# A deeper ring for expert rows: nine places, eight fetches asked ahead, and the dot written over its own rows

## The chip, the cores and the metric

The kernel runs on one core of a Trainium2 chip. Its five engines are told by the names of the profile: PE (TensorE), DVE (VectorE), ACT (ScalarE), POOL (GpSimd) and SP (SyncE); each works through its own list of instructions in order. The metric is the device time of one execution in microseconds (us), lower is better. The kernel before takes 1699.54 us (median of three runs, 1698.48 to 1712.32).

## The reference

Two layers work on 256 tokens of width 1024. Each layer has a mixer (gated linear attention beside spatial gating, one input projection, one output projection), a residual norm, an expert retrieval and another residual norm:

```python
h = _layer_norm(x, ln_in_g, ln_in_b)
for l in range(DEPTH):                                  # 2
    h = _layer_norm(ALPHA * h + _mixer(h, ...), ln1_g[l], ln1_b[l])
    h = _layer_norm(ALPHA * h + _peer(h, ...), ln2_g[l], ln2_b[l])

def _peer(x, ...):       # per token: 8 heads x top 16 = 128 experts of 16384
    ...                  # q = x @ wq, product keys, two rounds of top_k
    ub = jnp.take(u_tab, ib, axis=0)
    act = jax.nn.gelu(jnp.einsum('td,tkd->tk', xb, ub), approximate=False)
    vb = jnp.take(v_tab, ib, axis=0)
    return jnp.einsum('tk,tkd->td', gb * act, vb)
```

For each token and each of its 128 experts, a row u of 1024 numbers is fetched and multiplied with the token (a dot), the result goes through GELU and a gate, and a row v of 1024 numbers, times that weight, is added up.

## The kernel before

**The expert stream.** The 256 tokens are two blocks (b = 0, 1) of 128, one token to a partition. With two layers that makes four stretches of 128 expert steps, K = 128 and N = 512 steps in all, in the order (layer 0, b 0), (layer 0, b 1), (layer 1, b 0), (layer 1, b 1). Step k of a stretch handles the k-th expert of all 128 tokens:
- `gather` (line 726): one indirect DMA, issued by POOL, fetches for each token a row of 2048 floats (u beside v, 8 KB a partition, 1 MB in all) into a `uv` tile. The tiles are a ring of UVBUFS = 7 places.
- `dot` (line 733): one DVE instruction multiplies the u half with the token's row of `h` and sums it into `dots`; the products themselves go to a tile `junk` that nothing reads.
- `weigh` (lines 739 to 742): three ACT instructions make GELU, the gate, and `dg`, a diagonal matrix of the weights.
- the product (line 791): TensorE multiplies `dg` with the v half, two halves of 512 columns (x2 in the lists of the order, x4 in the profile), adding up in two `bank_acc` banks over the 128 steps.

A place of the ring is free for a new gather when its product is done.

**The side work.** Beside the steps of one stretch the kernel computes what the next stretch needs, a Python generator `side(n)`: the residual norm of the stretch that has just ended, the whole mixer of the next layer for that block (weights `raw` come over SP's DMA queue, ACT and DVE split each into two parts, `whi` on line 142 and `wlo` on line 147), then `ask`: the retrieval's queries, keys and rounds of top 16, nearly all of it small DVE instructions (lines 603 to 678). Each `yield` of a generator names a cost; the loop takes pieces until the cost passes PACE, then goes on to the next step. The last stretch has only a norm beside it.

**What sets the order.** DVE, ACT and PE run in the order in which the loop writes their instructions. In step i the loop writes: the gather of expert i + AHEAD - 1 (AHEAD = 5, so i + 4), the product of expert i - 2, the dot of expert i, the weighing of expert i - 1, then the pieces of side work. POOL's list holds the gathers and a few small powers for the norms (lines 161 and 215, `rs` and `rrs`), in the order of the program too.

Of the kernel before, what the change touches and what calls it, by code (L numbers as in the profile page):

```python
# [8 lines left out]
F32 = mybir.dt.float32  # L9
# [5 lines left out]
OP = mybir.AluOpType  # L15
# [6 lines left out]
D = 1024  # L22
# [11 lines left out]
NCAND = sum(na * nb for _, na, nb in RECTS)  # L34
NEG = -3.0e38
RAW, HI, LO = 4, 3, 2
UVBUFS, AHEAD = 7, 5
PACE = (1.65, 1.36, 1.36, 1.5)
OUTS = (4, 5, 6, 7, 0, 1, 2, 3)
HH = 2  # L40
# [59 lines left out]
class Trunk:  # L100
# [470 lines left out]
    def run(self):  # L571
        nc, a, sm = self.nc, self.a, self.sm
        with self.tc.tile_pool(name="peer", bufs=1) as pp:
# [108 lines left out]
            def ask(l, b, feed):  # L682

                S = pp.tile([128, PH, 2, NK], F32, name="S", tag="S")
                banks = [None]

                def query(i):
                    if i % 2 == 0:
                        banks[0] = self.bank("a")
                    p = self.wide(b, *feed.get(), banks[0][:, i % 2 * 256:(i % 2 + 1) * 256])  # L690
                    feed.split()
                    yield
                    s = pp.tile([128, 128], F32, name="f_half", tag="f_half", bufs=2)
                    nc.scalar.copy(s, p[1])  # L694
                    yield
                    q = pp.tile([128, 128], F32, name="qp", tag="qp", bufs=2)
                    nc.vector.tensor_tensor(q, p[0], s, op=OP.add)  # L697
                    yield
                    p2 = self.bank("b")[:, :128]
                    nc.tensor.matmul(p2, lhsT=q, rhs=kt[:, l, i % 2], start=True, stop=True)  # L700
                    yield
                    nc.scalar.copy(S[:, i // 2, i % 2], p2)
                    yield
                    h, half = divmod(i, 2)
                    top16((S[:, h, half], v16[:, h, half], i16[:, h, half]))
                    if i % (2 * HH) == 2 * HH - 1:
                        yield
                        yield from retrieve(l, h // HH)
                live = []
                todo = [query(i) for i in range(16)]  # L710
                while todo or live:
                    for w in list(live):
                        try:
                            next(w)
                        except StopIteration:
                            live.remove(w)
                    if todo:
                        w = todo.pop(0)
                        next(w)
                        live.append(w)  # L720
                    yield 2.9


            def gather(eid, k):
                uv = pp.tile([128, 2 * D], F32, name="uv", tag="uv", bufs=UVBUFS)
                nc.gpsimd.indirect_dma_start(out=uv, out_offset=None, in_=a["uv"],  # L726
                                             in_offset=bass.IndirectOffsetOnAxis(ap=eid[:, k:k + 1], axis=0),
                                             bounds_check=L * NK * NK - 1, oob_is_err=False)
                return uv

            def dot(b, k, uv, dots):
                junk = pp.tile([128, D], F32, name="junk", tag="junk")
                nc.vector.scalar_tensor_tensor(junk, uv[:, :D], 1.0, self.h[:, b], op0=OP.mult, op1=OP.mult,  # L733
                                               accum_out=dots[:, k:k + 1])

            def weigh(k, ex, dots):

                c = dots[:, k:k + 1]
                nc.scalar.activation(c, c, AF.Gelu)  # L739
                nc.scalar.mul(c, c, ex[:, k:k + 1])  # L740
                dg = pp.tile([128, 128], F32, name="dg", tag="dg", bufs=3)
                nc.scalar.mul(dg, self.ident, c)  # L742
                return dg

            chosen, ready = [], set()
            def side(n, done):

                if n == 0:
                    yield from asked
                    nc.sync.dma_start(self.h[:, 1], a["x"][128:256, :])  # L750
                    feed = self.feed_of(0)
                    yield 0.1
                    yield from self.input_block(1)
                    yield from self.front(pp, 0, 1, feed)
                    yield from ask(0, 1, feed)
                elif n < 3:
                    b = n - 1
                    feed = self.feed_of(1)
                    yield from self.residual_block(done, b, V_LN2)
                    if b == 0:  # L760
                        self.layer_constants(pp, 1)
                    yield from self.front(pp, 1, b, feed)
                    yield from ask(1, b, feed)
                else:
                    yield from self.output_block(done, 0, V_LN2 + V_LAYER)

            with self.tc.manual_schedule(engines=ORDERED):
                for _ in self.input_block(0):
                    pass
                for _ in self.front(pp, 0, 0, feed):  # L770
                    pass
                asked = ask(0, 0, feed)
                while (0, 0) not in ready:
                    next(asked)


                K = PH * TK
                N = NB * L * K
                uvs, dgs = {}, {}
                work, debt, acc = None, 0.0, None  # L780
                for i in range(N + 2):
                    for j in range(0 if i == 0 else i + AHEAD - 1, min(i + AHEAD, N)):
                        while (j // K, j % K // KH) not in ready:
                            next(work)
                        uvs[j] = gather(chosen[j // K][0], j % K)
                    if i > 1:
                        m = i - 2
                        if m % K == 0:
                            acc = [self.bank("acc") for _ in range(2)]
                        for hf in range(2):  # L790
                            nc.tensor.matmul(acc[hf], lhsT=dgs[m], rhs=uvs[m][:, D + hf * 512:D + (hf + 1) * 512],  # L791
                                             start=m % K == 0, stop=m % K == K - 1)
                        del dgs[m], uvs[m]
                    if i < N:
                        dot(i // K % NB, i % K, uvs[i], chosen[i // K][2])
                    if 0 < i <= N:
                        dgs[i - 1] = weigh((i - 1) % K, *chosen[(i - 1) // K][1:])
                    if i == 0 or (i > 2 and i % K == 1 and i < N):
                        for _ in work or []:
                            pass  # L800
                        work, debt = side(i // K, acc), 0.0
                    if work:
                        debt += PACE[min(i // K, 3)]
                        while debt > 0:
                            c = next(work, work)
                            if c is work:
                                break
                            debt -= c or 1.5
                for _ in self.output_block(acc, 1, V_LN2 + V_LAYER):
                    pass  # L810

# [86 lines left out]
```

## Time and profile before

| what | value |
|---|---|
| median of three runs | 1699.54 us |
| the profiled execution's own time | 1692.46 us |
| its span in the profile | 1690.7 us |
| PE, DVE, ACT, POOL busy | 85%, 71%, 47%, 36% of the span |
| moved by DMA | 636.60 MB, 377 GB/s in the mean |
| share of the 16 DMA engines: gathers, weights | 78.3%, 15.3% |
| gathers, dots, products | 512 each |

The busy shares are means over stages with different limits. A row of the windows view tells what an engine did in one stretch of time; a row of the waits view tells who kept an engine idle. Times in them count from the start of the span.

### The profile page before, as it was taken

Reading aid. Unit: us, or ns where it says so; the run is one execution under the profiler, and the core shown is the slowest. Engines: PE = TensorE matmul, PEld = TensorE weight load, DVE = VectorE, ACT = ScalarE, POOL = GpSimd, SP = SyncE. Lnnn points to the kernel's source line nnn. Section 1 sums busy time; section 2 is a strip of 40 time slices with the busy share of each in tenths; the row PEclk is TensorE's granted clock in tenths of the full one; section 3 lists DMA queues with packets and bytes.
Section 4 is the critical chain, followed back from the end, with each engine's and each line's share of the span. In section 5 each row is a group of like instructions: output and inputs, shape, how many; then the busy total and the mean of one; then the engine's idle time right before and its main releaser. Section 6 shows DMA issues by size and latency. Waiting matters only on the chain.

```text
span 1690.7 us, 17829 instructions
## 1 busy us (share of the span) xinstructions
PE 1430.4 (85%) x4544; PEld 749.1 (44%) x4544; DVE 1204.0 (71%) x2898; ACT 794.7 (47%) x2106; POOL 614.1 (36%) x542
## 2 busy tenths in 40 slices
PE   7887699989878889989887798989977887777776
PEld 5675255646533455445543354545543332222222
DVE  6778977767998667666898566766899654444444
ACT  5643465654544565544444374544444433333332
POOL 0002343444324343444334343444324433333331
PEclk9976999999899999999999898999989989999999
DMA  7647999999989999999989999999989999999996
GB/s 234 224 143 300 347 390 396 416 417 419 404 330 364 392 418 391 419 419 419 396 353 386 402 399 363 418 419 419 419 320 361 409 372 421 422 421 422 421 421 255
DMA packets 102409, 636.60 MB, mean 377 GB/s; under 512 B 11634, under 2 KB 12436, under 8 KB 36772
## 3 DMA queue, kind: packets, MB, share of 16 engines
q0 software_dynamic: 73872, 537.49, 78.3%
q1 hardware_dynamic: 28436, 97.98, 15.3%
q8 instruction: 37, 0.61, 0.1%
q14 instruction: 64, 0.52, 0.1%
HBM read 634.38 MB, written 1.05 MB: 376 GB/s over the span
## 4 chain that ended last, share of the span: by engine, by line
DVE 28%; DMA 24%; issue 19%; PE 14%; POOL 12%; ACT 2%; POOLq 1%; DVEq 0%; SPq 0%; ACTq 0%
DMA uv<-uv,eid 23%; POOL uv L726 11%; DVE junk L733 10%; PE bank_acc L791 7%; PE bank_a L153 5%; DVE wlo L147 3%; DVE i L605 2%; DVE v L603 2%; PE bank_b L179 1%; DVE S L608 1%; DVE sums L650 1%; POOLq L726 1%; DVE pos L605 1%; DVE sums L651 1%; ACT whi L142 1%
## 5 line engine op out<-in xcount | busy, mean ns | idle before, releaser
L791 PE MATMUL bank_acc<-uv,dg 128*128 128x512 f32 x2048 | 1012.3, 629 | 199.0 <-ACT dg L742 187.7
L726 POOL DMA_INDIRECT uv<-uv,eid x512 | 595.8, 1164 | 917.8 <-PE bank_acc L791 599.1
L733 DVE SCALAR_TENSOR_TENSOR junk<-uv,h 128x1024 f32<-128x1024 f32 x512 | 626.8, 1224 | 369.6 <-DMA uv<-uv,eid 364.6
L791 PEld LDWEIGHTS bank_acc<-uv,dg 128*128 128x128 f32 x2048 | 375.6, 196 | 723.4 <-ACT dg L742 383.9
L739 ACT ACTIVATE dots<-dots 128x1 f32<-128x1 f32 x512 | 103.3, 202 | 561.1 <-DVE junk L733 556.6
L147 DVE TENSOR_TENSOR wlo<-raw,whi 128x1024 fp32r<-128x1024 f32 x180 | 218.9, 1219 | 35.0 <-issue 16.9
L742 ACT ACTIVATE dg<-ident,dots 128x128 f32<-128x128 f32 x512 | 205.6, 402 | 38.5 <-PE bank_acc L791 21.9
L142 ACT CAST whi<-raw 128x1024 fp32r<-128x1024 f32 x180 | 187.4, 1044 | 42.9 <-DMA raw<-wmix 23.6
L740 ACT ACTIVATE dots<-dots,ex 128x1 f32<-128x1 f32 x512 | 150.8, 295 | 16.6
L153 PE MATMUL bank_a<-whi,x 128*128 128x512 f32 x384 | 137.2, 465 | 6.4 <-ACT f_sr L520 4.8
L153 PE MATMUL bank_a<-x,whi 128*128 128x256 f32 x672 | 118.9, 325 | 9.3 <-ACT f_half L694 6.1
L153 PEld LDWEIGHTS bank_a<-x,whi 128*128 128x128 f32 x672 | 98.2, 213 | 24.6 <-issue 9.8
L153 PEld LDWEIGHTS bank_a<-whi,x 128*128 128x128 f32 x384 | 72.7, 192 | 48.0 <-issue 27.4
L153 PE MATMUL bank_a<-x,wlo 128*128 128x128 f32 x672 | 91.1, 282 | 0.0
L153 PEld LDWEIGHTS bank_a<-x,wlo 128*128 128x128 f32 x672 | 89.5, 206 | 0.0
L179 PE MATMUL bank_b<-vecs,ident 16*128 16x512 f32 x96 | 58.9, 752 | 23.8 <-DVE f_at L408 11.9
L694 ACT COPY f_half<-bank_a 128x128 f32<-128x128 f32 x64 | 17.0, 265 | 113.6 <-DVE qp L697 109.1
L153 PE MATMUL bank_a<-wlo,x 128*128 128x512 f32 x192 | 66.6, 401 | 2.0 <-DVE wlo L147 1.9
L700 PEld LDWEIGHTS bank_b<-kt,qp 128*128 128x128 f32 x128 | 26.0, 214 | 40.6 <-issue 17.1
L179 PEld LDWEIGHTS bank_b<-vecs,ident 16*128 16x128 f32 x96 | 19.5, 219 | 55.2 <-issue 30.2
L153 PEld LDWEIGHTS bank_a<-wlo,x 128*128 128x128 f32 x192 | 36.3, 191 | 13.3 <-DVE wlo L147 5.2
L733 DVE DVE_READ_ACCUMULATOR junk<-uv,h 128x1 f32 x512 | 42.1, 82 | 0.0
(137 smaller groups left out, 761.6 us busy)
## 6 DMA issues: line engine op xcount, KB each, us to landing
raw<-wmix SPq DMA_DIRECT2D x180, 512.0 KB
uv<-uv,eid POOLq DMA_INDIRECT x512
h<-x SPq DMA_DIRECT2D x2, 512.0 KB
out<-h SPq DMA_DIRECT2D x4, 256.0 KB
f_cM<-gm POOLq DMA_DIRECT2D x1, 576.0 KB
f_sw<-sgwT SPq DMA_DIRECT2D x2, 256.0 KB
f_msk<-gmask SPq DMA_DIRECT2D x1, 320.0 KB
kt<-kT SPq DMA_DIRECT2D x2, 128.0 KB
```

The source lines that it names most:

```text
L142: self.nc.scalar.copy(hi, raw)
L147: self.nc.vector.tensor_tensor(lo, raw, hi.bitcast(F32), op=OP.subtract)
L153: self.nc.tensor.matmul(out, lhsT=l, rhs=r, start=start and i == 0, stop=stop and i == n - 1)
L179: self.nc.tensor.matmul(p, lhsT=self.ident[0:16, row:row + 1].to_broadcast([16, 128]), rhs=self.vecs[:, hf * 512:(hf + 1) * 512], start=Tr ...
L603: nc.vector.max(v[:, r], vals)
L605: nc.vector.max_index(i[:, r], v[:, r], vals)
L726: nc.gpsimd.indirect_dma_start(out=uv, out_offset=None, in_=a["uv"], in_offset=bass.IndirectOffsetOnAxis(ap=eid[:, k:k + 1], axis=0), boun ...
L733: nc.vector.scalar_tensor_tensor(junk, uv[:, :D], 1.0, self.h[:, b], op0=OP.mult, op1=OP.mult, accum_out=dots[:, k:k + 1])
L739: nc.scalar.activation(c, c, AF.Gelu)
L740: nc.scalar.mul(c, c, ex[:, k:k + 1])
L742: nc.scalar.mul(dg, self.ident, c)
L791: nc.tensor.matmul(acc[hf], lhsT=dgs[m], rhs=uvs[m][:, D + hf * 512:D + (hf + 1) * 512], start=m % K == 0, stop=m % K == K - 1)
```

## The change

The ring gets nine places, and in step i the loop writes the gather of expert i + 7, where it was i + 4. The dot writes its products over the u half that it has just read, and the tile `junk` is gone. The product of expert i - 1 is now written at the end of step i, behind the side work, where the product of i - 2 was written at the start of step i before. The side work of a stretch starts one step after the stretch's first dot; before, that held for all but the first stretch, whose side work started with its first dot.

```diff
--- before.py
+++ after.py
@@ -34,7 +34,7 @@
 NCAND = sum(na * nb for _, na, nb in RECTS)
 NEG = -3.0e38
 RAW, HI, LO = 4, 3, 2
-UVBUFS, AHEAD = 7, 5
+UVBUFS, AHEAD = 9, 8
 PACE = (1.65, 1.36, 1.36, 1.5)
 OUTS = (4, 5, 6, 7, 0, 1, 2, 3)
 HH = 2
@@ -729,8 +729,8 @@
                 return uv

             def dot(b, k, uv, dots):
-                junk = pp.tile([128, D], F32, name="junk", tag="junk")
-                nc.vector.scalar_tensor_tensor(junk, uv[:, :D], 1.0, self.h[:, b], op0=OP.mult, op1=OP.mult,
+                u = uv[:, :D]
+                nc.vector.scalar_tensor_tensor(u, u, 1.0, self.h[:, b], op0=OP.mult, op1=OP.mult,
                                                accum_out=dots[:, k:k + 1])

             def weigh(k, ex, dots):
@@ -778,34 +778,33 @@
                 N = NB * L * K
                 uvs, dgs = {}, {}
                 work, debt, acc = None, 0.0, None
-                for i in range(N + 2):
+                for i in range(N + 1):
                     for j in range(0 if i == 0 else i + AHEAD - 1, min(i + AHEAD, N)):
                         while (j // K, j % K // KH) not in ready:
                             next(work)
                         uvs[j] = gather(chosen[j // K][0], j % K)
-                    if i > 1:
-                        m = i - 2
-                        if m % K == 0:
-                            acc = [self.bank("acc") for _ in range(2)]
-                        for hf in range(2):
-                            nc.tensor.matmul(acc[hf], lhsT=dgs[m], rhs=uvs[m][:, D + hf * 512:D + (hf + 1) * 512],
-                                             start=m % K == 0, stop=m % K == K - 1)
-                        del dgs[m], uvs[m]
                     if i < N:
                         dot(i // K % NB, i % K, uvs[i], chosen[i // K][2])
-                    if 0 < i <= N:
+                    if i > 0:
                         dgs[i - 1] = weigh((i - 1) % K, *chosen[(i - 1) // K][1:])
-                    if i == 0 or (i > 2 and i % K == 1 and i < N):
+                    if i > 0 and (i - 1) % K == 0:
                         for _ in work or []:
                             pass
-                        work, debt = side(i // K, acc), 0.0
+                        work, debt = side((i - 1) // K, acc), 0.0
+                        acc = [self.bank("acc") for _ in range(2)]
                     if work:
-                        debt += PACE[min(i // K, 3)]
+                        debt += PACE[min((i - 1) // K, 3)]
                         while debt > 0:
                             c = next(work, work)
                             if c is work:
                                 break
                             debt -= c or 1.5
+                    if i > 0:
+                        m = i - 1
+                        for hf in range(2):
+                            nc.tensor.matmul(acc[hf], lhsT=dgs[m], rhs=uvs[m][:, D + hf * 512:D + (hf + 1) * 512],
+                                             start=m % K == 0, stop=m % K == K - 1)
+                        del dgs[m], uvs[m]
                 for _ in self.output_block(acc, 1, V_LN2 + V_LAYER):
                     pass

```

How the instructions then stand: POOL's first gathers and what each waits for (in brackets: `DMASW0` to `DMASW7` are eight counters, one of which each of POOL's DMAs raises when it has landed, in turn; `DVE` and `PE` mean a wait for an instruction of that engine). Before:

```order
L726 DMA uv<-uv,eid 128x2048 [waits DVE_49]
L726 DMA uv<-uv,eid 128x2048 x6
L726 DMA uv<-uv,eid 128x2048 [waits DMASW0_49,DMASW1_49,DVE_49,PE_49]
L726 DMA uv<-uv,eid 128x2048 [waits DMASW2_49,DVE_49,PE_49]
L726 DMA uv<-uv,eid 128x2048 [waits DMASW3_49,DVE_49,PE_49]
```

and now:

```order
L726 DMA uv<-uv,eid 128x2048 [waits DVE_49]
L726 DMA uv<-uv,eid 128x2048 x6
L726 DMA uv<-uv,eid 128x2048 [waits DMASW0_49]
L726 DMA uv<-uv,eid 128x2048 [waits DMASW1_49]
L726 DMA uv<-uv,eid 128x2048 [waits DMASW2_49,DVE_49,PE_49]
```

Before, the eighth gather was the first that waited for a dot and a product; now it is the tenth, and the eighth and ninth wait only for the landing of an earlier DMA of POOL, eight DMAs back.

On PE, in the first stretch, where the queries' key products (line 700) are side work. Before:

```order
L153 MATMUL bank_a<-x,wlo 128x128 x8
L700 MATMUL bank_b<-kt,qp 128x128
L153 MATMUL bank_a<-x,whi 128x256 x8
L153 MATMUL bank_a<-x,wlo 128x128 x8
L791 MATMUL bank_acc<-uv,dg 128x512 x4
L700 MATMUL bank_b<-kt,qp 128x128
L153 MATMUL bank_a<-x,whi 128x256 x8
```

and now:

```order
L153 MATMUL bank_a<-x,wlo 128x128 x8
L805 MATMUL bank_acc<-uv,dg 128x512 x2
L700 MATMUL bank_b<-kt,qp 128x128
L153 MATMUL bank_a<-x,whi 128x256 x8
L153 MATMUL bank_a<-x,wlo 128x128 x8
L805 MATMUL bank_acc<-uv,dg 128x512 x4
L700 MATMUL bank_b<-kt,qp 128x128
```

The first expert's product (the first row of `bank_acc`, x2) now stands ahead of a key product that it stood behind. On PE in the third stretch, where the norm of the ended stretch (lines 179 and 188) and the next layer's first projections (line 153) stand among the products. Before:

```order
L179 MATMUL bank_b<-vecs,ident 128x512 x4
L791 MATMUL bank_acc<-uv,dg 128x512 x2
L188 MATMUL bank_b<-ident,h 128x128 x8
L791 MATMUL bank_acc<-uv,dg 128x512 x4
L153 MATMUL bank_a<-x,whi 128x256 x8
L153 MATMUL bank_a<-x,wlo 128x128 x8
L791 MATMUL bank_acc<-uv,dg 128x512 x2
```

and now:

```order
L179 MATMUL bank_b<-vecs,ident 128x512 x4
L805 MATMUL bank_acc<-uv,dg 128x512 x2
L188 MATMUL bank_b<-ident,h 128x128 x8
L805 MATMUL bank_acc<-uv,dg 128x512 x4
L153 MATMUL bank_a<-x,whi 128x256 x8
L153 MATMUL bank_a<-x,wlo 128x128 x8
L805 MATMUL bank_acc<-uv,dg 128x512 x2
```

Nothing moved there but the product's line number. Outside the first stretch, the lists of PE, DVE and ACT are the same in the same order.

## Rows read from the trace of the kernel before

**Rows 1.** The page's first line.

```profile
span 1690.7 us, 17829 instructions
```

**Rows 2.** Windows: start:end, busy us (x instructions) by engine, PEclk, DMA share, GB/s.

```profile
140.00:240.00 100.00, 77.01 (x223) 39.30 (x224) 88.87 (x299) 45.72 (x122) 40.13 (x35) 0.86 0.95 366
...
300.00:440.00 140.00, 132.16 (x501) 78.17 (x500) 103.86 (x215) 73.93 (x195) 58.91 (x47) 0.98 1.02 418
440.00:540.00 100.00, 76.46 (x240) 38.66 (x239) 93.48 (x338) 45.37 (x126) 35.34 (x31) 0.91 0.91 352
...
560.00:600.00 40.00, 36.22 (x141) 21.10 (x141) 29.21 (x51) 25.21 (x62) 14.08 (x12) 0.91 0.97 388
...
640.00:660.00 20.00, 20.00 (x67) 11.71 (x65) 14.84 (x27) 14.18 (x31) 9.16 (x7) 0.99 0.94 361
...
820.00:920.00 100.00, 77.43 (x244) 39.98 (x244) 95.19 (x343) 45.14 (x126) 34.66 (x31) 0.91 0.94 369
...
960.00:980.00 20.00, 20.00 (x65) 10.51 (x63) 13.45 (x23) 9.15 (x28) 6.73 (x6) 0.79 0.87 337
...
1020.00:1060.00 40.00, 32.98 (x104) 18.34 (x103) 27.05 (x47) 19.99 (x47) 12.35 (x10) 0.87 0.89 360
...
1220.00:1320.00 100.00, 75.91 (x243) 39.17 (x242) 95.19 (x340) 45.42 (x128) 36.15 (x31) 0.93 0.90 349
...
1360.00:1380.00 20.00, 20.00 (x35) 8.17 (x34) 10.12 (x16) 5.06 (x18) 6.97 (x7) 0.73 0.83 317
1380.00:1660.00 280.00, 222.70 (x450) 75.94 (x448) 138.14 (x224) 100.57 (x336) 111.78 (x114) 1.00 1.01 421
```

**Rows 3.** DVE's waits, in 300:440, 440:540 and 1380:1660: us in total, times, longest.

```profile
DVE junk L733 <- DMA uv<-uv,eid: 33.4, 26, 2.5
...
DVE junk L733 <- DMA uv<-uv,eid: 0.5, 1, 0.5
...
DVE junk L733 <- DMA uv<-uv,eid: 143.5, 112, 3.0
```

**Rows 4.** Timeline in the last stretch: start, us, instruction [idle before it <-releaser].

```profile
1499.44 0.99 POOL L726 DMA_INDIRECT uv<-uv,eid  x1 [1.50 <-PE bank_acc L791]
...
1499.87 1.23 DVE L733 SCALAR_TENSOR_TENSOR junk<-uv,h 128x1024 f32<-128x1024 f32 x1 [1.25 <-DMA uv<-uv,eid]
...
1501.93 0.99 POOL L726 DMA_INDIRECT uv<-uv,eid  x1 [1.50 <-PE bank_acc L791]
...
1502.15 1.98 PE L791 MATMUL bank_acc<-uv,dg 128*128 128x512 f32 x4 [0.50 <-ACT dg L742]
1502.35 1.22 DVE L733 SCALAR_TENSOR_TENSOR junk<-uv,h 128x1024 f32<-128x1024 f32 x1 [1.25 <-DMA uv<-uv,eid]
```

**Rows 5.** POOL's waits in 440:540, columns as in rows 3.

```profile
POOL uv L726 <- PE bank_b L700: 16.5, 5, 7.2
POOL uv L726 <- PE bank_acc L791: 16.3, 9, 5.2
POOL uv L726 <- DVE qp L697: 7.8, 1, 7.8
```

**Rows 6.** Timeline of POOL around 1030.

```profile
1026.92 1.59 POOL L726 DMA_INDIRECT uv<-uv,eid  x1 [0.23 <-issue]
1040.72 1.00 POOL L726 DMA_INDIRECT uv<-uv,eid  x1 [12.21 <-PE bank_acc L791]
```

**Rows 7.** A group of line 733, and the instructions of line 522 (min/median/max ns).

```profile
L733 DVE SCALAR_TENSOR_TENSOR junk<-uv,h 128x1024 f32<-128x1024 f32 x512 | 626.8, 1224 | 369.6 <-DMA uv<-uv,eid 364.6 <-issue 1.2
...
L522 DVE TENSOR_TENSOR f_sr<-f_sr,f_gg x4: 686/688/694, 68.9 to 1096.0; 128x512 f32<-128x512 f32 x4
```

**Rows 8.** Timeline at the start of the third stretch.

```profile
958.58 3.34 PE L791 MATMUL bank_acc<-uv,dg 128*128 128x512 f32 x4 [4.45 <-issue]
...
961.23 0.56 POOL L215 TENSOR_TENSOR rrs<-rve,mhalf 128x1 f32<-128x1 f32 x1 [5.84 <-DVE rve L548]
...
965.68 1.40 DVE L232 SCALAR_TENSOR_TENSOR h<-h,rrs,bank_b 128x512 f32<-128x512 f32 x2
```

## The prediction

> **What bounds the kernel now.** The first view to read is the table of windows [rows 2], cut where its character changes, with the span [rows 1] beside it. The last stretch, 1380 to 1660, has nothing but expert steps and moves 421 GB/s with the DMA share at 1.01; its DVE waits 143.5 us for gathers in 112 waits [rows 3]. The mixed stretch 300 to 440, with weights and side work beside the experts, moves 418 GB/s, and there too DVE waits for rows (33.4 us). In these stretches the transfers are the bound, and 418 GB/s is what they reach with weights among them; the long stretches 660 to 820 and 1060 to 1220, whose rows are not shown, read the same. The kernel therefore gets shorter only where the transfers run below that. Rows 2 has nine such places, and the lost time of each is its length times (1 - rate / 418):
> - four long ones, beside the rounds of top 16: 140 to 240 at 366 GB/s, 12.4 us lost; 440 to 540 at 352, 15.8 us; 820 to 920 at 369, 11.7 us; 1220 to 1320 at 349, 16.5 us;
> - five short ones: 560 to 600 at 388, 2.9 us; 640 to 660 at 361, 2.7 us; 960 to 980 at 337, 3.9 us; 1020 to 1060 at 360, 5.6 us; 1360 to 1380 at 317, 4.8 us.
> Together 76.3 us, the most that any change of the ring can bring without moving fewer bytes.
>
> Why are the transfers idle there? In the long ones DVE is busy 93 to 95 of 100 us (89 in the first) and waits 0.5 us for rows between 440 and 540 [rows 3], so the rows lie there and DVE is the bound: the ring is full. In the short ones TensorE is late: from 960 and from 1360 PE is busy 20.00 of 20 us at a mean granted clock of 0.79 and 0.73, so partly at the lower of its two levels, 1.2 GHz, and before the first of these it had stood idle for 4.45 us [rows 8]; one POOL wait for a product lasts 12.21 us before the gather at 1040.72, the first since 1026.92 [rows 6]. Both are the same fault seen from the transfers: no place is free, so nothing is asked for.
>
> **The change, part by part.** *Two more places.* One gather takes 1501.93 - 1499.44 = 2.49 us of a saturated DMA [rows 4]. Two more places let the transfers run 2 x 2.49 = 5.0 us further into each idle place before the ring is full again. A long place keeps its own length, as DVE's work sets it, but leaves with two more experts landed, and the stretch after it, which is bound by transfers, ends 5.0 us earlier. A short one that lost less than 5.0 us loses nothing. So: 4 x 5.0 = 20.0 us for the long ones, and 2.9 + 2.7 + 3.9 + 5.0 + 4.8 = 19.3 us for the short ones, 39.3 us in all.
>
> *Is a gain of two places real on POOL?* The lists in the section on the change show a wait that looks like a limit: each gather also waits for the landing of POOL's DMA eight before it. In [rows 4] the dot at 1499.87 starts when its rows have landed; its product, at 1502.15, ends at 1504.13, 4.3 us after that landing, and the next rows land 2.48 us after the first (dot at 1502.35). So the landing of the gather eight back comes 4.3 - 2.5 = 1.8 us ahead of the product nine back, and where DVE or PE are behind, far more. The product's wait ends last, and the ring does count nine.
>
> *The dot over its own rows.* The same 512 instructions read and write the same number of elements [rows 7], 1224 ns each; only the address of the write changes, so a gain is excluded. No dot of before writes onto its own SBUF input. The nearest row is the multiplication of line 522, which does: 688 ns for 512 elements. Twice that, with its fixed cost counted twice, is 1376 ns, so the upper end is 1376 - 1224 = 152 ns a dot. It would matter only where DVE is the bound: POOL issues 35 + 31 + 31 + 31 = 128 gathers in the four long places, about as many dots, 128 x 0.152 = 19 us. I take 0, as half of the 688 ns must hold a fixed part as well. The place is freed by the product, which comes behind the dot anyhow, so the new write adds no wait to the next gather.
>
> *The product one step behind its dot.* From the lists: the same order on PE, DVE and ACT in the second to fourth stretch. In the first, each product stands one step earlier against the side work, as the side work and its loads on SP's queue start a step later. Nothing is added; a place comes free slightly sooner, the side work ends a step later, and as written its last expert list is ready in step 116 of 128, before 115. I take 0, inside a bound of one gather, 2.5 us, either way.
>
> *Powers behind deeper gathers.* POOL's list has 13 small powers of the norms with gathers behind them. Such a power now stands behind gather i + 7, which waits for the product of expert i - 2; before, behind i + 4 and the product of i - 3. It is later by up to a product (3.34 us at the third stretch's start, 958.58) and a gather of 0.99 us. There the product ends at 961.92, so the power would start about 963.2 instead of 961.23; its reader on DVE, line 232, starts at 965.68 [rows 8]. The 3.9 us between end and reader cover 2 us, so 0. If the cover were gone, up to 3.34 + 0.99 = 4.3 us at each of 13, see the rivals. In the other direction, POOL used to sit at a power with only four experts asked ahead and now has seven, which is part of what fills the short places.
>
> *Sum.* 1692.46 - 39.3 = 1653.2 us for an execution like the profiled one. That one is 7.1 us below the median of 1699.54 us that the change is measured against, so the forecast is 1699.54 - 39.3 = **1660 us**, 2.3% less.
>
> **Rivals.**
> *Nothing in the long places.* POOL writes the fetch commands, and if DVE holds POOL up there, a deeper ring changes nothing in them: 1699.5 - 19.3 = 1680 us. For it: between 440 and 540 some of POOL's waits are put down to DVE (7.8 us to line 697 alone) [rows 5]. Against: 32.8 us are put down to PE (16.5 and 16.3), and DVE has rows waiting all the time. A rule of the skill bears on this: the Trainium skill, "SBUF — State Buffer", section "SBUF: two separate sides", says that a GpSimd DMA stands still while DVE holds their common port, since its descriptors cannot be written. By it alone the sum would be 19.3 us; by the row of DVE's waits, 0.5 us in 100, late descriptors cost nothing there, and I follow the row. Chance 0.12.
>
> *The consumers never catch up.* Two more experts landed are worth something only if DVE and PE then work them off faster than they come; if not, the ring stays full from one idle place to the next, and it pays once for several. DVE's 33.4 us of waits from 300 to 440 speak against it; for it, PE is busy 132 of 140 us there. If the reserve paid only once in each of the four stretches, 4 x 5.0 = 20 us at best and 10 us if half of that is worked off: 1680 to 1690 us, at 1688. Chance 0.11.
>
> *One place instead of two,* if the landing counter or the in-place write holds the ninth: half of each long place, 10 us, and 2.5 us of each short one, 12.5 us: 1677 us. Chance 0.07.
>
> *Slower: the powers come late.* If line 232 and its like do wait for their power, DVE stands, and the dots behind it. It decides from the point at which a power ends after 965.68 in [rows 8], that is 3.9 us later than now. Then 13 x 4.3 = 56 us are added, and the short places, which follow such powers, gain nothing; the long ones still give 20.0 us: 1699.5 + 56 - 20 = 1735 us. Chance 0.04.
>
> *More than the two places,* because the transfers, idle less often, also lose less in starting again: half of the 37 us that the sum leaves, 18 us, 1642 us. Chance 0.08.
>
> **How the numbers follow.** The forecast keeps 0.58. Its own range is the 39.3 us less the dot's 19 us at worst, and a few us more at best: 1655 to 1679. The range is drawn to 1643 and 1683 us: it takes in the one-place and no-long-place rivals and leaves out the slower one, most of the second rival and about half of the last. A change within 1%, 17 us, is about what a measurement cannot tell from none. Faster by over 1% means below 1682.5: nearly all of the forecast, the first, third and last rival for the most part and little of the second, 0.79. Within 1%: 0.16. Slower: 0.05.
>
> **What the profile of the changed kernel would show.** The saturated stretches stay at 418 and 421 GB/s. The long places still have DVE busy near 95% and lose about 5 us less each; the short ones near 560, 640, 960 and 1360 are gone, and the 12.21 us of POOL before a gather turn into some 7 us or less. The dot's mean stays at 1224 ns, bytes and gathers stay as they are. I would be wrong if the dot got longer, if powers were followed by DVE waits for POOL, or if the short places stayed as deep as now.

## The result, and the profile after

The changed kernel takes 1656.46 us (median of four runs, 1649.67 to 1660.02); the kernel before took 1699.01 us in the same comparison (four runs). The ratio is 0.9739 with a 95% interval of 0.9681 to 0.9796: 2.6% faster, 42.6 us by the medians (the ratio is not the quotient of the two medians, which would be 0.9750). The forecast was 1660 us.

The profiled execution after took 1658.65 us. First its windows, cut so that each answers to a row of [rows 2]; the idle places come earlier from one to the next, as time is saved.

```profile
140.00:240.00 100.00, 74.96 (x231) 38.84 (x231) 88.77 (x309) 44.67 (x120) 45.89 (x37) 0.88 0.98 387
300.00:440.00 140.00, 131.80 (x506) 78.47 (x505) 104.15 (x217) 71.78 (x190) 63.56 (x48) 0.99 1.02 417
440.00:540.00 100.00, 78.60 (x239) 39.58 (x238) 92.92 (x339) 47.34 (x134) 39.06 (x32) 0.88 0.95 372
560.00:600.00 40.00, 40.00 (x146) 22.56 (x145) 28.89 (x48) 23.64 (x59) 18.50 (x12) 0.87 0.93 363
640.00:660.00 20.00, 20.00 (x69) 11.79 (x68) 15.56 (x30) 13.45 (x32) 8.78 (x8) 1.00 1.02 418
820.00:920.00 100.00, 80.28 (x237) 40.05 (x238) 94.60 (x331) 48.81 (x141) 43.24 (x34) 0.93 0.98 390
940.00:960.00 20.00, 18.08 (x51) 8.71 (x52) 14.61 (x29) 8.94 (x25) 6.05 (x5) 0.83 1.02 419
960.00:980.00 20.00, 20.00 (x94) 12.64 (x93) 14.71 (x25) 15.73 (x39) 11.51 (x7) 1.00 1.02 418
1020.00:1060.00 40.00, 40.00 (x139) 23.95 (x138) 29.24 (x53) 24.71 (x58) 18.30 (x14) 0.99 0.99 401
1200.00:1300.00 100.00, 77.03 (x240) 38.56 (x239) 95.63 (x346) 48.48 (x138) 41.77 (x33) 0.93 0.94 373
1340.00:1380.00 40.00, 36.82 (x81) 14.69 (x79) 20.17 (x34) 15.85 (x55) 23.52 (x21) 0.98 1.01 420
1380.00:1620.00 240.00, 189.60 (x383) 65.02 (x384) 118.13 (x191) 85.33 (x285) 94.82 (x96) 1.00 1.01 421
```

The last column is the one to read. The saturated stretches are what they were, 417 and 421 GB/s. The four long places rise from 366, 352, 369 and 349 to 387, 372, 390 and 373 GB/s, while DVE stays as busy as in [rows 2]. By the prediction's formula, length times (1 - rate / 418), they now lose 7.4, 11.0, 6.7 and 10.8 us, that is 5.0, 4.8, 5.0 and 5.7 us less than before. Of the short places, those near 640, 960 and 1360 are gone (418 to 420 GB/s); the one from 1020 is down from 5.6 to 1.6 us; the one from 560 is up from 2.9 to 5.3 us. The sum is 20.5 + 13.0 = 33.5 us, and the spans differ by 1690.7 - 1656.9 = 33.8 us. The table of windows accounts for nearly all of it; two things outside it almost cancel. One is a tenth place that [rows 2] does not show, 280 to 300. It lost 2.2 us before and nothing after:

```profile
280.00:300.00 20.00, 19.61 (x59) 11.21 (x60) 12.43 (x20) 11.63 (x26) 6.00 (x5) 0.86 0.95 371
...
280.00:300.00 20.00, 19.20 (x63) 11.30 (x64) 14.78 (x26) 13.78 (x32) 7.06 (x5) 1.00 1.01 417
```

The other is the first gather, which starts 2.3 us later (141.40 us, where it was 139.06). The medians differ by more because the profiled execution of before was 6.5 us below its median and that of after 2.2 us above.

The dots, from the groups of the profile after, beside [rows 7]; and DVE's waits for its rows between 440 and 540, beside [rows 3]:

```profile
L733 DVE SCALAR_TENSOR_TENSOR uv<-uv,h 128x1024 f32<-128x1024 f32 x512 | 619.0, 1223 | 332.0 <-DMA uv<-uv,eid 329.7 <-PE bank_acc L805 1.2 <-issue 0.2
...
DVE uv L733 <- DMA uv<-uv,eid: 2.3, 1, 2.3
```

Their mean is 1223 ns, where it was 1224. DVE still finds its rows landed in a long place: one wait of 2.3 us, at its very end (538 us).

POOL's timeline where [rows 6] showed the 12.21 us wait:

```profile
1003.65 1.46 POOL L726 DMA_INDIRECT uv<-uv,eid  x1 [0.30 <-PE bank_b L398]
1006.48 0.56 POOL L161 TENSOR_TENSOR bnrs<-rs,mhalf 128x1 f32<-128x1 f32 x1 [1.38 <-DVE rs L160]
1021.35 1.04 POOL L726 DMA_INDIRECT uv<-uv,eid  x1 [14.30 <-PE bank_acc L805]
```

That wait is now 14.30 us, longer, and yet the transfers lost 1.6 us there instead of 5.6: POOL has asked for everything that the ring has room for and then sits, while the transfers still have gathers to work off.

And the timeline at the place of [rows 8]:

```profile
941.92 3.40 PE L805 MATMUL bank_acc<-uv,dg 128*128 128x512 f32 x4 [3.76 <-issue]
...
945.60 0.99 POOL L726 DMA_INDIRECT uv<-uv,eid  x1 [6.17 <-PE bank_acc L805]
946.61 0.58 POOL L215 TENSOR_TENSOR rrs<-rve,mhalf 128x1 f32<-128x1 f32 x1
...
949.28 1.40 DVE L232 SCALAR_TENSOR_TENSOR h<-h,rrs,bank_b 128x512 f32<-128x512 f32 x2
```

The power now starts right behind a gather that waited for the product just ended. It ends at 947.19, its reader on DVE starts at 949.28: the cover has shrunk from 3.9 us to 2.1 us, and the reader does not wait. In the whole execution DVE waits once for POOL, for 0.9 us, and it does so before the change too.

### The profile page after: what moved, and what is told of

Read it like the earlier page. It is cut to its first block, busy times and chain, and to the rows that moved or that the text cites. A ratio compares the mean times of both kernels' runs of the same rounds, so it can differ in the third digit from the quotient of the medians.

```text
span 1656.9 us, 17671 instructions
## 1 busy us (share of the span) xinstructions
PE 1418.7 (86%) x4544; PEld 749.1 (45%) x4544; DVE 1195.5 (72%) x2898; ACT 794.2 (48%) x2106; POOL 650.8 (39%) x542
## 4 chain that ended last, share of the span: by engine, by line
DMA 29%; DVE 28%; issue 17%; PE 17%; POOL 5%; ACT 3%; POOLq 0%; DVEq 0%; SPq 0%; ACTq 0%
DMA uv<-uv,eid 27%; DVE uv L733 10%; PE bank_acc L805 8%; PE bank_a L153 6%; POOL uv L726 5%; DVE wlo L147 3%; DVE i L605 2%; PE bank_b L179 2%; DVE v L603 2%; DMA raw<-wmix 1%; DVE S L608 1%; ACT whi L142 1%; DVE sums L650 1%; DVE sums L651 1%; DVE qp L697 1%
## 5 line engine op out<-in xcount | busy, mean ns | idle before, releaser
L805 PE MATMUL bank_acc<-uv,dg 128*128 128x512 f32 x2048 | 1000.2, 625 | 183.2 <-ACT dg L742 172.5
L726 POOL DMA_INDIRECT uv<-uv,eid x512 | 633.5, 1237 | 878.9 <-PE bank_acc L805 585.8
L733 DVE SCALAR_TENSOR_TENSOR uv<-uv,h 128x1024 f32<-128x1024 f32 x512 | 619.0, 1223 | 332.0 <-DMA uv<-uv,eid 329.7
L147 DVE TENSOR_TENSOR wlo<-raw,whi 128x1024 fp32r<-128x1024 f32 x180 | 219.0, 1220 | 45.7 <-issue 22.5
L733 DVE DVE_READ_ACCUMULATOR uv<-uv,h 128x1 f32 x512 | 42.6, 83 | 0.0
L191 ACT CAST x<-bank_b 128x512 fp32r<-128x512 f32 x24 | 13.7, 584 | 59.7 <-PE bank_b L188 59.5
```

Of the source, the lines that this page charges most:

```text
L147: self.nc.vector.tensor_tensor(lo, raw, hi.bitcast(F32), op=OP.subtract)
L733: nc.vector.scalar_tensor_tensor(u, u, 1.0, self.h[:, b], op0=OP.mult, op1=OP.mult, accum_out=dots[:, k:k + 1])
```

## The experiments

The theory: a place of the ring lets the transfers run one gather (2.5 us) further into every place where their consumers stand, and the number of places is the whole gain. The rivals: the product's new place in the loop, the dot over its own rows, asking further ahead past the small powers, or a better rate of the transfers everywhere. All times are medians beside the kernel before on the same chip; ratios are to that kernel, with 95% intervals.

**Seven places in the changed loop.**

```diff
-UVBUFS, AHEAD = 9, 8
+UVBUFS, AHEAD = 7, 6
```

> The changed kernel with seven places and six experts asked ahead; the dot over its own rows and the new place of the product stay. If the two extra places are the whole gain, it runs like the kernel before, 1699 us within 0.5%. If the product's new place or the dot over its own rows gives the gain, it stays near 1656 us; if the dot costs its upper bound, it is up to 19 us slower than before.

1700.17 us against 1696.57; ratio 1.002 (0.9995 to 1.0045). The loop's new order and the dot's new target, without the two places, bring nothing.

**Eight places.**

```diff
-UVBUFS, AHEAD = 9, 8
+UVBUFS, AHEAD = 8, 7
```

> The changed kernel with eight places and seven asked ahead. If each place is worth one gather (2.5 us) in each of the nine idle places, half of the long ones' 20.0 us and 2.5 us in each of five short ones: 22.5 us, 1676 us. If only the ninth place counts, or the step from seven to eight already gives all, it is 1699 or 1656 us.

1670.59 us; ratio 0.9822 (0.9791 to 0.9853): 26 us less than the kernel before by the medians, 30 us by the ratio. That is more than the 22.5 us expected, so the first extra place was undersized and the second, some 13 us by the ratios, oversized (16.8 us expected). The extra came from the short places: they lost 26 to 33 us in the profiles with seven places and 14 us in this one (the table in the last section).

**The dot over its own rows alone.** The kernel before with

```diff
-                junk = pp.tile([128, D], F32, name="junk", tag="junk")
-                nc.vector.scalar_tensor_tensor(junk, uv[:, :D], 1.0, ...
+                u = uv[:, :D]
+                nc.vector.scalar_tensor_tensor(u, u, 1.0, ...
```

> The kernel before with one edit, the dot written over its own rows (seven places, five asked ahead, the old loop). If the write costs and brings nothing, 1699 us within 0.5% and a mean dot of 1224 ns; if it costs up to 152 ns a dot, up to 1718 us.

1695.6 us; ratio 0.9992 (0.9966 to 1.0018). Its group of dots:

```profile
L733 DVE SCALAR_TENSOR_TENSOR uv<-uv,h 128x1024 f32<-128x1024 f32 x512 | 620.8, 1223 | 372.4 <-DMA uv<-uv,eid 369.8 <-PE bank_acc L791 1.8
```

1223 ns: writing over its own input costs DVE nothing.

**Nine places in the old loop.** The same in-place dot in the kernel before, and

```diff
-UVBUFS, AHEAD = 7, 5
+UVBUFS, AHEAD = 9, 7
```

> The kernel before with nine places and the dot over its own rows, but the old loop: the product of expert i - 2 at the start of step i, seven asked ahead (the most that this order of the program has places for). If the places are the whole gain, 1656 us as the changed kernel, within 0.5%. If the product one step behind its dot gives a part, it is slower than that by the part; if it gives all, 1699 us.

1653.96 us; ratio 0.9724 (0.9687 to 0.976), the changed kernel's own ratio. The product's new place adds nothing to the places.

**Ten places.** The changed kernel with

```diff
-UVBUFS, AHEAD = 9, 8
+UVBUFS, AHEAD = 10, 9
-                S = pp.tile([128, PH, 2, NK], F32, name="S", tag="S")
+                S = pp.tile([128, PH, 2, NK], F32, name="S", tag="m2")
```

> Ten places and nine experts asked ahead; the 8 KB a partition that this takes come from the score tile S, which shares its place with the attention tile m2 (their uses never overlap). If a further place is worth one more gather wherever the transfers still idle, 4 x 2.5 us in the long places, and 2.5 + 1.6 us in the two short ones that are left near 560 and 1020: 14 us less than the changed kernel, 1642 us. If the eight landing counters hold the tenth place, or the short ones are all that was to be had, it stays at 1656 us.

1646.06 us against 1694.31; ratio 0.9726 (0.9679 to 0.9774). This was 11 us below the next experiment, which has nine places on the same chip, but the interval overlapped that of the changed kernel; the last pair settles it.

**Five asked ahead with nine places.**

```diff
-UVBUFS, AHEAD = 9, 8
+UVBUFS, AHEAD = 9, 5
```

> The changed kernel with nine places, but only five experts asked ahead, as before. The number only says where in POOL's list the small powers stand among the gathers, so if the places are the gain, the long ones keep their 20 us, and of the short ones, which follow powers, a part of 19 us goes: 1656 to 1670 us. If asking further ahead is what gives the gain, it is 1699 us. If powers behind deeper gathers cost something in the changed kernel, it is faster than 1656 us.

1656.97 us; ratio 0.9787 (0.974 to 0.9835). The interval holds the changed kernel's ratio too, so five and eight experts asked ahead cannot be told apart: neither a gain from asking further ahead nor a cost of the powers behind deeper gathers is seen, though a few us either way would not show.

**The long places without their cause.** Retrieval cut down on DVE, with seven and with nine places: for each score list the second round becomes a copy of the first, and the three rounds of comparing and adding up (lines 656 to 671) become plain copies. It fetches other experts, as many:

```diff
-top16((S[:, h, half], v16[:, h, half], i16[:, h, half]))
+nc.vector.max(v[:, 0:8], vals)
+nc.vector.max_index(ix[:, 0:8], v[:, 0:8], vals)
+nc.vector.tensor_copy(v[:, 8:16], v[:, 0:8])
+nc.vector.tensor_copy(ix[:, 8:16], ix[:, 0:8])
...
+for e in range(2):
+    nc.vector.tensor_copy(idx[:, e].rearrange("p (h k) -> p h k", h=HH), k12[:, :, e])
```

> Seven places (six asked ahead), and about a third of DVE's work beside the four long places left out: the second round of top 16 over the scores is replaced by a copy of the first, and the expert numbers are made from the first 16 keys instead of the chosen pairs. It fetches other experts, as many. If DVE holds the long places, the 56 us lost in them go and about 10 us of the first list before the first gather: 1699 - 66 = 1633 us, and the rates there rise from 349 to 369 GB/s to 400 or more. If POOL's writing of the fetch commands or the transfers themselves hold them, it stays above 1680 us.

1638.78 us against 1694.31; ratio 0.9689 (0.964 to 0.9738). Some 15 of these 55.5 us come from ahead of the stream, as the first gather starts at 123.69 us instead of 139.06. Windows of three of its long places (the second, third and fourth of before):

```profile
420.00:520.00 100.00, 83.94 (x252) 39.51 (x251) 70.89 (x238) 50.53 (x145) 42.72 (x37) 0.97 1.01 419
780.00:880.00 100.00, 81.64 (x275) 41.87 (x275) 76.04 (x272) 51.78 (x146) 43.12 (x36) 0.98 1.01 419
1160.00:1260.00 100.00, 86.19 (x306) 46.00 (x306) 77.77 (x277) 52.61 (x150) 46.90 (x38) 0.98 1.01 412
```

With DVE busy 71 to 78 of 100 us instead of 93 to 95, the transfers run at 412 to 419 GB/s with seven places. DVE was what held them. The cut takes away DVE's work and with it any hold that DVE has on POOL, so it does not tell these two apart; the windows after do, as there a deeper ring gains in the long places with DVE as busy as before.

> The same cut with nine places (eight asked ahead). If the long places give 20 of the gain through DVE, only the short ones' share is left between this and the seven places with the cut: 15 to 23 us less. If the deeper ring works everywhere, by a better rate of the transfers, the distance stays at 43 us.

1618.4 us; ratio 0.9559 (0.951 to 0.9609). Nine places are worth 20.4 us here instead of 42.6: without the long places, their part of the gain is gone.

**Six places.**

```diff
-UVBUFS, AHEAD = 9, 8
+UVBUFS, AHEAD = 6, 5
```

> The changed kernel with six places and five experts asked ahead, one place fewer than the kernel before. If a place is worth one gather in each idle place, the nine give up 2.5 us each and places that were hidden so far appear: at least 22 us more, 1718 us or above. If seven places were already short of some other limit that six do not touch, it stays near 1696 us.

1720.36 us against 1694.89; ratio 1.0129 (1.0082 to 1.0177). One place fewer than before costs 22 us by the ratio and 25 us by the medians, a little less than the first extra place gives.

**The shared tile alone,** with nine places:

```diff
-                S = pp.tile([128, PH, 2, NK], F32, name="S", tag="S")
+                S = pp.tile([128, PH, 2, NK], F32, name="S", tag="m2")
```

> The changed kernel, nine places and eight asked ahead, with S in the place of m2 and nothing else, the control for the ten places. If sharing the place costs and brings nothing, 1655 us, as the changed kernel; if the sharing itself gave the gain of the ten places, 1646 us.

1653.62 us; ratio 0.9743 (0.971 to 0.9776), as the changed kernel. What ten places gain is not the sharing.

**Nine and ten places side by side.** The changed kernel and the kernel with ten places, unchanged from above, on one chip.

> The changed kernel itself, beside ten places on the same chip and the same runs of the kernel before: 0.974 of the kernel before.

1655.18 us against 1697.87; ratio 0.9743 (0.9719 to 0.9767).

> Ten places with the shared tile, beside the changed kernel. If the tenth place still fills 2.5 us in each long place, at least 8 us less than nine places and an interval clear of theirs; if the landing counters, for which POOL waited 162 us in the first run of ten places, hold it, less than 3 us.

1640.61 us; ratio 0.9668 (0.9646 to 0.9689), clear of nine places by 14.6 us. Ten places beat both kernels. POOL's waits in it, and its timeline in the last stretch, beside [rows 4]:

```profile
POOL uv L726 <- PE bank_acc L805: 354.7, 182, 14.3
POOL uv L726 <- DMA uv<-uv,eid: 159.7, 133, 4.4
```

```profile
1499.83 1.23 DVE L733 SCALAR_TENSOR_TENSOR uv<-uv,h 128x1024 f32<-128x1024 f32 x1 [1.25 <-DMA uv<-uv,eid]
1500.50 1.42 POOL L726 DMA_INDIRECT uv<-uv,eid  x1 [1.06 <-DMA uv<-uv,eid]
...
1502.98 1.42 POOL L726 DMA_INDIRECT uv<-uv,eid  x1 [1.06 <-DMA uv<-uv,eid]
```

Here the landing counter does end last: 159.7 us of POOL's waits are for the landing of the gather eight back, 1.06 us before each gather of this stretch. It costs nothing there, as the gathers still follow each other 2.48 us apart, the pace of the saturated transfers.

## Why the prediction was right

**What bounds the kernel.** Right. Where the transfers ran at 418 to 421 GB/s before, they run at 417 to 421 after, and the 33.8 us between the spans come out of the idle places. The list of nine was one short: 280 to 300, at 371 GB/s, is a tenth and adds 2.2 us to the 76.3 us and to the sum.

**Two more places, the long ones.** Right in mechanism, and in these windows in size: 20.5 us for 20.0 forecast. Counted in finer windows (the table in the last section), the changed kernel's two profiles lose 12 to 17 us less in the long places than the three with seven, and 20 to 28 us less in the short ones. So the sum holds better than its two parts, and that it came out so close is partly luck. That DVE sets the long places is shown by the cut: with less DVE work the places vanish and with them half of what nine places are worth.

**Two more places, the short ones.** Right in mechanism, the size off: 13.0 us in the profile for 19.3. Three are gone as forecast. The one from 1020 kept 1.6 us. The one from 560 was forecast to lose nothing and lost 5.3 us. PE's rows at this place, of the kernel before and of the changed kernel:

```profile
563.85 1.96 PE L791 MATMUL bank_acc<-uv,dg 128*128 128x512 f32 x4 [3.78 <-issue]
565.73 4.15 PE L179 MATMUL bank_b<-vecs,ident 16*128 16x512 f32 x8
```

```profile
553.95 3.75 PE L805 MATMUL bank_acc<-uv,dg 128*128 128x512 f32 x4 [3.78 <-issue]
557.63 7.19 PE L179 MATMUL bank_b<-vecs,ident 16*128 16x512 f32 x8
```

PE stands idle for 3.78 us in both, and then the same instructions take nearly twice as long after. The windows from 540 to 610 show the granted clock (third from the end) and the rate: the kernel before, the changed kernel, its second profile (from the run side by side with ten places), nine places in the old loop, and seven in the changed loop:

```profile
540.00:610.00 70.00, 63.09 (x204) 32.15 (x203) 45.31 (x77) 36.51 (x97) 28.34 (x25) 0.95 0.99 403
540.00:610.00 70.00, 65.78 (x206) 34.41 (x205) 45.54 (x77) 41.46 (x102) 33.49 (x24) 0.88 0.97 388
540.00:610.00 70.00, 65.91 (x209) 34.09 (x207) 47.48 (x82) 41.68 (x103) 33.48 (x25) 0.90 1.00 403
540.00:610.00 70.00, 65.72 (x228) 36.66 (x227) 50.67 (x89) 44.09 (x105) 32.34 (x24) 0.95 1.01 418
540.00:610.00 70.00, 63.21 (x196) 31.42 (x195) 41.69 (x73) 34.39 (x90) 31.69 (x24) 0.90 0.93 372
```

All five spend some of this time at TensorE's lower level (1.2 GHz, half of full speed): a mean of 0.95 over 70 us is 7 us of it, 0.90 is 14 us, 0.88 is 17 us. By the formula they lose 2.5, 5.0, 2.5, 0.0 and 7.7 us. At equal clocks two more places save 2.5 us (all there was, at 0.95) and 5.2 us (at 0.90), as forecast; at equal places the loss grows with the time at the lower level, in two profiles of one and the same kernel too. So two places were worth here what the forecast said, but it took the place to stay as long as in the profile before, and in the profile after it was longer. No run set the clock by itself, and what keeps it down for longer in some executions is open. A part of the loss after also follows a gather that occupies POOL for 5.12 us, unknown to the kernel before (see the last section):

```profile
577.59 5.12 POOL L726 DMA_INDIRECT uv<-uv,eid  x1 [1.73 <-PE bank_acc L805]
583.02 0.99 POOL L726 DMA_INDIRECT uv<-uv,eid  x1 [0.30 <-issue]
```

The next gather starts only at 583.02, and from 580 to 600 the transfers run at 381 GB/s, 1.8 us lost. That the long gather is the cause of these 1.8 us is not shown.

**The ring counts nine on POOL.** Right: the product nine back ends last, and only with a tenth place does the landing eight back take over, as the 1.8 us of the prediction would have it (a tenth place moves the product 2.49 us further back).

**The dot over its own rows.** Right at 0: 1223 ns, and the kernel before with this edit alone runs as before. The upper bound of 152 ns a dot was far too wide.

**The product one step behind its dot.** Right at 0, shown from both sides: the new loop with seven places gains nothing, the old loop with nine gains all.

**Powers behind deeper gathers.** Right at 0: the cover shrank from 3.9 to 2.1 us and held. The aside that asking further ahead past the powers is a part of the gain was not borne out: five asked ahead cannot be told from eight.

**The signs.** Two were wrong. The place near 560 was to be gone and is not. The 12.21 us wait was to become some 7 us and became 14.30. The places have no part in that: the wait is 14.3 to 14.8 us in the changed loop with seven, eight, nine and ten places, 12.2 to 12.6 us in the old loop with seven and nine, and 10.0 us with nine places and five asked ahead. A wait of POOL for a place measures how long the consumers stand, not how long the transfers do.

**The rivals.** Nothing in the long places, by commands that POOL cannot write: refuted by the windows after, where each long place loses less with DVE as busy. That DVE's hold on POOL costs nothing at all there is not shown. Consumers that never catch up: refuted by 4.8 to 5.7 us in each long place and the saturated stretches of the table back at 417 to 421 GB/s. One place instead of two: refuted by eight places against nine. The slower case: no wait for a power appeared. More than two places' worth: by the medians 3.3 us more than forecast, by the profile 5.5 us less, so none of it is shown.

## What to carry to other kernels

Where a stream of transfers is the bound in most stretches and its consumers in some, a ring's depth is worth one transfer's time for each stretch in which the consumers stand, and never more than that stretch loses: so count such stretches in a table of rates that leaves no part of the span out, price them, and cap each. The rate of the transfers by window shows the loss; waits for a free place do not. Memory is the price of a place, so a scratch output that nobody reads, or two tiles that are never alive together, are where to look for it.

## What the runs showed of the hardware

The time follows the number of places: ratio 1.0129 for six, 1.002 for seven, 0.9822 for eight, 0.9743 for nine, 0.9668 for ten. The rate of the saturated transfers does not: in the last stretch it is 421 GB/s with six, seven, nine and ten.

Where the places act, by the profiles: cut from 150 us to the last 60 us into windows of 10 us, with each window under 414 GB/s counted at its lost time, and as part of a long place where DVE is busy 85% or more:

| places | profiles | lost in long places, us | lost in short ones, us |
|---|---|---|---|
| 6 | 1 | 62.3 | 50.8 |
| 7 | 3 | 46.9 to 52.5 | 25.8 to 33.0 |
| 8 | 1 | 44.2 | 14.0 |
| 9 | 5 | 33.7 to 37.9 | 3.5 to 6.2 |
| 10 | 2 | 23.8 to 24.8 | 1.1 |

With ten places the short ones are used up; the long ones still lose some 6 us each.

In every kernel here with the in-place dot two gathers in each execution, the fourteenth of the second stretch and the fourteenth of the third in the changed kernel, occupy POOL for 5.12 to 5.13 us (3.99 us with six places); before, the longest of 512 took 2.33 us. One of the changed kernel:

```profile
961.04 5.13 POOL L726 DMA_INDIRECT uv<-uv,eid  x1 [1.62 <-PE bank_acc L805]
```

What they wait for is open. The rate of the transfers was 418 GB/s around this one, so it cost nothing there; behind the one at 577.59 it fell, as told above.
